# A mixture-of-experts layer: x of expert 0 in two transfers, of the even and of the odd partitions

## The chip, the cores and the metric

The kernel runs on one core of a Trainium2 chip. The core has five engines that run their own instruction streams: TensorE (PE) multiplies matrices, VectorE (DVE) and ScalarE (ACT) do elementwise work, GpSimd (POOL) and SyncE (SP) here mainly issue transfers. Sixteen DMA engines move data between the chip's memory (HBM) and the on-chip SBUF, which has 128 partitions. The metric is the time of one execution in device microseconds: 179.32 us before, the median of 3 runs (179.29 to 179.36).

## The reference

```python
def setup_inputs():
    n_experts, capacity, hidden, expert_hidden = 8, 256, 512, 2048
    ...
def reference(x, w1, w2):
    h = np.matmul(x, w1)
    h = np.maximum(h, 0)
    return np.matmul(h, w2).astype(np.float32)
```

For each of 8 experts, x is 256 x 512, w1 512 x 2048 and w2 2048 x 512, all float32. x is 4.2 MB in all, the weights are 67.1 MB and the result is 4.2 MB.

## The kernel before, in words

The kernel has no planner: each engine's instructions are written out, and semaphores order the engines.

**Loads.** GpSimd casts to bfloat16 while it loads. It first issues x of experts 4 to 7 (`x_c`, L154), then w1 and w2, one transfer of 4.2 MB of float32 for each matrix (`load_w1` L144, `load_w2` L149; the last w2 in two pieces, L151 and L152). There are two buffers for w1 and two for w2; a transfer for a later expert waits until the expert before it in that buffer has been used. SyncE loads x of experts 0 to 3 as float32 into `x_f` in three transfers at L97: expert 0, then experts 1 and 2 together, then expert 3. Each has a semaphore of its own, `s_x[0]` to `s_x[2]`; a landed transfer adds 16 to it. Expert 0 is laid out with rows 2p and 2p+1 in partition p, so each partition gets 4 KB that lie in one piece in HBM.

**The barrier.** After these three issues the kernel closes its tile context (L103 and L104), which puts a barrier over all engines there. What GpSimd, ACT, DVE and PE do for the kernel comes behind that barrier, GpSimd's transfers too.

**Turning x.** For each pair of experts `take_x` runs on two engines at once: DVE takes the experts with b = 0 and ACT those with b = 1. Each waits for its x, casts it to bfloat16 in `x_b` (`cast`, L187), lets TensorE transpose the 16 blocks of the pair (L285) and copies the result to `xe` (L203, L213, L216). TensorE waits for both casts before it transposes a pair. DVE's first cast is the only reader of x of expert 0; its wait is the one in `take_x` with r = 0 and b = 0.

**The layers.** For each pair of experts TensorE runs layer 1 of both (L301; ReLU on DVE L235 and ACT L233) and then layer 2 of both (L321; copies to `out_sb` at L244). TensorE takes one unit of the semaphore `t_w` before each expert's layer 1 and before layer 2. SyncE gives these units: it waits for a weight's landing (L121 for w1, L130, L132 and L133 for w2) and then adds to `t_w`.

**Stores.** SyncE stores experts 0 to 5 in one transfer at L126, expert 6 and expert 7 in one each at L136, and at the end waits for all three landings (L332).

Of the kernel before, what the change touches and what calls it, by code (L numbers as in the profile page):

```python
# [9 lines left out]
def kernel(  # L10
# [8 lines left out]
    P = 128  # L19
# [25 lines left out]
    x_r = x.rearrange("e (p m) k -> p e m k", m=MT)  # L45
# [4 lines left out]
    x_f = nc.alloc_sbuf_tensor("x_f", [P, G, MT, H], f32)  # L50
# [16 lines left out]
    s_x = [sem(f"s_x{i}") for i in range(3)]  # L67
# [21 lines left out]
    sp, pool, act, dve, pe = nc.sync, nc.gpsimd, nc.scalar, nc.vector, nc.tensor  # L89
# [3 lines left out]

    def load_x(eng, e, n, src, i):
        ins = eng.dma_start(x_f[:, e:e + n], src).then_inc(s_x[i], 16)  # L97
        return ins.ins.name

    tc.no_tile_sem_insts.add(load_x(sp, 0, 1, x_r[:, :1], 0))  # L100
    tc.no_tile_sem_insts.add(load_x(sp, 1, 2, x_pair, 1))
    tc.no_tile_sem_insts.add(load_x(sp, G - 1, 1, x_r[:, G - 1:G], 2))
    tc.close()  # L103
    tc.compile()  # L104
# [77 lines left out]
    def cast(eng, r, b):  # L182

        a = 2 * r + b
        src = x_f[:, a] if a < G else x_c[:, MT * (a - G):MT * (a - G + 1)]
        copy = act.copy if eng is act else dve.tensor_copy
        copy(  # L187
            x_b[:, b].rearrange("p (t m) q -> p t m q", m=MT),
            src.rearrange("p m (q t) -> p t m q", t=KT1),
        ).then_inc(t_xb, 1)  # L190

    def take_x(eng, b):
        copy = act.copy if eng is act else dve.tensor_copy
        for r in range(G):
            if r < G // 2:
                eng.wait_ge(s_x[(2 * r + b + 1) // 2], 16)
            elif r == G // 2:
                eng.wait_ge(s_xc, 16)
            cast(eng, r, b)
            eng.wait_ge(s_tr, 2 * r + b + 1)  # L200
            a, n = 2 * r + b, KT1 * C
            if a in (0, G - 1):
                copy(  # L203
                    xe[:, a * n:(a + 1) * n].rearrange("p (j f r) -> p j f r", f=2, r=R),
                    pt[b][:].rearrange("p j (r f) -> p j f r", f=2),
                ).then_inc(s_xe[b], 1)
            else:
                e0, l = (1, 2) if a < G else (G, G)
                f, i = (a - e0) % 2, (a - e0) // 2
                xl = xe[:, e0 * n:(e0 + 2) * n].rearrange(  # L210
                    "p (l j f q i) -> p l j f q i", l=2, j=KT1 * MT, f=2, i=l // 2)
                xp = pt[b][:].rearrange("p j (l q) -> p j l q", l=l)
                ins = copy(xl[:, :, :, f, :, i].rearrange("p l j q -> p j l q"), xp[:, :, :2])  # L213
                if l == G:
                    xl = xe[:, (E - 2) * n:].rearrange("p (l j q f) -> p l j q f", l=2, j=KT1 * MT, f=l)
                    ins = copy(xl[:, :, :, :, a - e0].rearrange("p l j q -> p j l q"), xp[:, :, 2:])  # L216
                ins.then_inc(s_xe[b], 1)
# [41 lines left out]

    act.sem_inc(t_ha, 1)  # L260
    take_x(act, 1)
    layers(act, 1, s_ha, s_oa, t_ha, s_act)

    dve.sem_inc(t_hb, 1)
    take_x(dve, 0)
    layers(dve, 0, s_hb, s_ob, t_hb, s_dve)

# [13 lines left out]
    with pe.Fori(0, G) as _r:  # L281
        take(t_xb, 2)
        for b in range(2):
            for j in range(KT1 * MT):
                ins = pe.transpose(pt[b][:, j], x_b[:, b, j], identity[:])  # L285
            ins.then_inc(s_tr, 1)

    with pe.Fori(0, G) as g:
        with pe.Fori(0, 2) as b:
            xs = ahead(xe, False, g * (4 * KT1 * C) + b * (2 * KT1 * C), [kt * C for kt in range(KT1)], C)  # L290
            take(t_w)
            with pe.Fori(0, NQ) as q:
                for i in range(FB):
# [6 lines left out]
                    for kt in range(KT1):  # L300
                        ins = pe.matmul(  # L301
                            ph[i // 2][:, i % 2, :],
                            ws[i % 2 * KT1 + kt],
                            xs[kt],
                            start=(kt == 0),
                            stop=(kt == KT1 - 1),
                        )
                    if i % 2:
                        ins.then_inc((s_hb, s_ha)[i // 2], 1)
        with pe.Fori(0, 2) as b:  # L310
            for kt in range(KT2):
# [8 lines left out]
                for m in range(MT):  # L320
                    ins = pe.matmul(  # L321
                        po[:, m],
                        hs[(kt - k0) * MT + m],
                        ws[kt - k0],
                        start=(kt == 0),
                        stop=(kt == KT2 - 1),
                    )
# [35 lines left out]
```

## Time and profile before

| what | value |
|---|---|
| median of 3 runs | 179.32 us |
| time of the profiled execution | 179.3 us |
| span of the profiled execution | 177.8 us |
| mean granted TensorE clock | 0.975 |
| PE busy | 129.4 us (73%) |
| DVE, ACT, POOL busy | 40.7, 40.1, 11.1 us |
| HBM read and written | 71.30 MB, 4.19 MB |

The span reaches from the first to the last instruction; the time of the execution has 1.5 us more around it. In the profile, PEld is TensorE's loading of weights, and SPq stands for SyncE's queue of instructions. GB/s of the DMA engines are counted by what is written, so a transfer that casts float32 to bfloat16 shows half of the bytes that it reads.

### The profile page before, as it was taken

Reading aid. Unit: us, or ns where it says so; the run is one execution under the profiler, and the core shown is the slowest. Engines: PE = TensorE matmul, PEld = TensorE weight load, DVE = VectorE, ACT = ScalarE, POOL = GpSimd, SP = SyncE. Lnnn points to the kernel's source line nnn. Section 1 sums busy time; section 2 is a strip of 40 time slices with the busy share of each in tenths; the row PEclk is TensorE's granted clock in tenths of the full one; section 3 lists DMA queues with packets and bytes.
Section 4 is the critical chain, followed back from the end, with each engine's and each line's share of the span. In section 5 each row is a group of like instructions: output and inputs, shape, how many; then the busy total and the mean of one; then the engine's idle time right before and its main releaser. Section 6 shows DMA issues by size and latency. Waiting matters only on the chain. (4 is left out here: it accounts for less than half of the span.)

```text
span 177.8 us, 2369 instructions
## 1 busy us (share of the span) xinstructions
PE 129.4 (73%) x824; PEld 87.8 (49%) x832; DVE 40.7 (23%) x56; ACT 40.1 (23%) x57; POOL 11.1 (6%) x24
## 2 busy tenths in 40 slices
PE   0034399897939697888769695979496695979890
PEld 0033388793413296773324485954142594944330
DVE  0142553331030333330200331320303132310100
ACT  2464543221020222130200222220202121310101
POOL 2600000101010001000010101010100200000000
PEclk9999999999996999999969999999999999999997
DMA  5999999999999999999999999999998999999998
GB/s 227 334 240 203 236 210 203 236 210 203 236 210 203 236 210 203 236 210 203 236 214 199 236 214 199 236 214 199 236 221 192 236 221 192 236 192 217 298 431 337
DMA packets 3712, 40.90 MB, mean 230 GB/s; under 512 B 384, under 2 KB 384, under 8 KB 1024
## 3 DMA queue, kind: packets, MB, share of 16 engines
q0 software_dynamic: 2592, 34.60, 91.5%
q1 hardware_dynamic: 1120, 6.29, 8.6%
HBM read 71.30 MB, written 4.19 MB: 425 GB/s over the span
## 5 line engine op out<-in xcount | busy, mean ns | idle before, releaser
L301 PE MATMUL pt_h<-xe,w_sb 128*128 x512 | 62.8, 276 | 12.5 <-PEq L92 12.4
L321 PE MATMUL pt_o<-w_sb,ht_sb 128*128 x248 | 59.4, 395 | 14.4 <-PEq L92 14.0
L301 PEld LDWEIGHTS pt_h<-xe,w_sb 128*128 x512 | 56.0, 146 | 19.9 <-issue 19.6
L321 PEld LDWEIGHTS pt_o<-w_sb,ht_sb 128*128 x256 | 25.3, 101 | 47.5 <-issue 21.0
L235 DVE TENSOR_SCALAR ht_sb<-pt_h 128x512 bf16<-128x512 f32 x32 | 22.1, 692 | 47.6 <-PE pt_h L301 47.6
L233 ACT ACTIVATE ht_sb<-pt_h 128x512 bf16<-128x512 f32 x32 | 19.1, 597 | 52.6 <-PE pt_h L301 52.6
L244 DVE COPY out_sb<-pt_o 64x512 f32 (+1 forms) x14 | 9.6, 689 | 68.9 <-PE pt_o L321 68.8
L244 ACT COPY out_sb<-pt_o 64x512 f32 (+1 forms) x14 | 8.1, 580 | 67.8 <-PE pt_o L321 67.7
L285 PE MATMUL pt_tr<-identity,x_b 128*128 128x128 bf16 x64 | 7.5, 310 | 16.9 <-PEq L92 16.9
L285 PEld LDWEIGHTS pt_tr<-identity,x_b 128*128 128x128 bf16 x64 | 6.5, 144 | 17.6 <-issue 17.6
L144 POOL DMA_DIRECT2D w_sb<-in_w_dram x8 | 5.0, 624 | 66.3 <-ACTq L237 66.3
L149 POOL DMA_DIRECT2D w_sb<-in_w_dram x7 | 3.7, 532 | 49.0 <-ACT out_sb L244 48.9
L187 ACT CAST x_b<-x_f 128x1024 bf16<-128x1024 f32 x2 | 4.0, 1988 | 2.3 <-DMA x_f<-in_x_dram 2.3
L213 DVE COPY xe<-pt_tr 128x512 bf16<-128x512 bf16 (+1 forms) x3 | 2.1, 715 | 7.9 <-PE pt_tr L285 7.9
L213 ACT COPY xe<-pt_tr 128x512 bf16<-128x512 bf16 (+1 forms) x3 | 2.5, 828 | 6.1 <-PE pt_tr L285 6.1
L187 DVE CAST x_b<-x_f 128x1024 bf16<-128x1024 f32 x2 | 2.1, 1067 | 4.1 <-DMA x_f<-in_x_dram 4.1
L216 ACT COPY xe<-pt_tr 128x512 bf16<-128x512 bf16 x2 | 2.7, 1336 | 0.0
L216 DVE COPY xe<-pt_tr 128x512 bf16<-128x512 bf16 x2 | 2.6, 1301 | 0.0
L203 DVE COPY xe<-pt_tr 128x1024 bf16<-128x1024 bf16 x1 | 1.2, 1225 | 4.5 <-PE pt_tr L285 4.5
L187 ACT COPY x_b<-x_c 128x1024 bf16<-128x1024 bf16 x2 | 2.3, 1132 | 0.0
L187 ACT ACT_TABLE_LOAD x1 | 1.3, 1283 | 2.9 <-PEq L104 2.9
L203 ACT COPY xe<-pt_tr 128x1024 bf16<-128x1024 bf16 x1 | 1.0, 1012 | 2.0 <-PE pt_tr L285 2.0
(10 smaller groups left out, 4.0 us busy)
## 6 DMA issues: line engine op xcount, KB each, us to landing
w_sb<-in_w_dram POOLq DMA_DIRECT2D x15, 2048.0 KB, 29.8
out_dram<-out_sb SPq DMA_DIRECT2D x1, 3072.0 KB, 9.8
w_sb<-in_w_dram POOLq DMA_DIRECT2D x1, 1152.0 KB, 25.7
x_f<-in_x_dram SPq DMA_DIRECT2D x2, 512.0 KB, 5.1
x_f<-in_x_dram SPq DMA_DIRECT2D x1, 1024.0 KB, 5.3
x_c<-in_x_dram POOLq DMA_DIRECT2D x1, 1024.0 KB, 9.4
out_dram<-out_sb SPq DMA_DIRECT2D x2, 512.0 KB, 6.1
w_sb<-in_w_dram POOLq DMA_DIRECT2D x1, 896.0 KB, 29.4
```

Source lines behind the costliest of these rows:

```text
L144: pool.dma_start(w1_k[:, e % 2 * KT1:(e % 2 + 1) * KT1], w1_r[e]).then_inc(s_w1[e], 16)
L149: pool.dma_start(w2_k[:, k:k + KT2], w2_r[e]).then_inc(s_w2[e], 16)
L187: copy(x_b[:, b].rearrange("p (t m) q -> p t m q", m=MT), src.rearrange("p m (q t) -> p t m q", t=KT1),).then_inc(t_xb, 1)
L203: copy(xe[:, a * n:(a + 1) * n].rearrange("p (j f r) -> p j f r", f=2, r=R), pt[b][:].rearrange("p j (r f) -> p j f r", f=2),).then_inc(s_ ...
L213: ins = copy(xl[:, :, :, f, :, i].rearrange("p l j q -> p j l q"), xp[:, :, :2])
L216: ins = copy(xl[:, :, :, :, a - e0].rearrange("p l j q -> p j l q"), xp[:, :, 2:])
L233: act.activation(dst, ph[half][:], relu).then_inc(t_h, 1)
L235: dve.tensor_relu(dst, ph[half][:]).then_inc(t_h, 1)
L244: ins = copy(dst, src)
L285: ins = pe.transpose(pt[b][:, j], x_b[:, b, j], identity[:])
L301: ins = pe.matmul(ph[i // 2][:, i % 2, :], ws[i % 2 * KT1 + kt], xs[kt], start=(kt == 0), stop=(kt == KT1 - 1),)
L321: ins = pe.matmul(po[:, m], hs[(kt - k0) * MT + m], ws[kt - k0], start=(kt == 0), stop=(kt == KT2 - 1),)
```

## The change

Expert 0's x comes in two transfers of 64 partitions each: first the even partitions 0, 2, 4, ..., then the odd ones. Both add to the same semaphore, and DVE's first wait asks for 32 in place of 16. Nothing else is edited.

```diff
-    def load_x(eng, e, n, src, i):
-        ins = eng.dma_start(x_f[:, e:e + n], src).then_inc(s_x[i], 16)
+    def load_x(eng, e, n, src, i, rows=slice(0, P)):
+        ins = eng.dma_start(x_f[rows, e:e + n], src[rows]).then_inc(s_x[i], 16)
         return ins.ins.name
 
-    tc.no_tile_sem_insts.add(load_x(sp, 0, 1, x_r[:, :1], 0))
+    for odd in range(2):
+        tc.no_tile_sem_insts.add(load_x(sp, 0, 1, x_r[:, :1], 0, slice(odd, P, 2)))
     tc.no_tile_sem_insts.add(load_x(sp, 1, 2, x_pair, 1))
     tc.no_tile_sem_insts.add(load_x(sp, G - 1, 1, x_r[:, G - 1:G], 2))
...
             if r < G // 2:
-                eng.wait_ge(s_x[(2 * r + b + 1) // 2], 16)
+                eng.wait_ge(s_x[(2 * r + b + 1) // 2], 32 if r + b == 0 else 16)
```

SyncE's instructions before, from the program's start to its stores (a branch stands where the program passes on, at L104 into the barrier):

```order
L358 UNCONDITIONAL_BRANCH
L97 DMA x_f<-in_x_dram 128x1024
L97 DMA x_f<-in_x_dram 128x2048
L97 DMA x_f<-in_x_dram 128x1024
L104 UNCONDITIONAL_BRANCH
L126 DMA out_dram<-out_sb 128x3x2048
L136 DMA out_dram<-out_sb 128x1024 x2
```

The same of the changed kernel, whose lines below L97 stand one further down:

```order
L359 UNCONDITIONAL_BRANCH
L97 DMA x_f<-in_x_dram 64x1024 x2
L97 DMA x_f<-in_x_dram 128x2048
L97 DMA x_f<-in_x_dram 128x1024
L105 UNCONDITIONAL_BRANCH
L127 DMA out_dram<-out_sb 128x3x2048
L137 DMA out_dram<-out_sb 128x1024 x2
```

In place of the first transfer stand two of 64 rows, so the other two transfers of x and the barrier come one instruction later on SyncE. The other engines have the same instructions in the same order.

## Rows read from the trace of the kernel before

**Rows 1.** The page: TensorE's busy time, DMA by slice (tenths busy), the queues.
```profile
PE 129.4 (73%) x824; PEld 87.8 (49%) x832; DVE 40.7 (23%) x56; ACT 40.1 (23%) x57; POOL 11.1 (6%) x24
...
DMA  5999999999999999999999999999998999999998
DMA packets 3712, 40.90 MB, mean 230 GB/s; under 512 B 384, under 2 KB 384, under 8 KB 1024
...
q0 software_dynamic: 2592, 34.60, 91.5%
q1 hardware_dynamic: 1120, 6.29, 8.6%
HBM read 71.30 MB, written 4.19 MB: 425 GB/s over the span
```

**Rows 2.** Windows of the span; the last columns are DMA share and GB/s.
```profile
core 0: us, PE busy (x) PEld busy (x) DVE busy (x) ACT busy (x) POOL busy (x), PEclk, DMA share, GB/s
1.60:1.80 0.20, 0.00 (x0) 0.00 (x0) 0.00 (x0) 0.00 (x0) 0.00 (x0) 1.00 0.22 41
1.80:2.00 0.20, 0.00 (x0) 0.00 (x0) 0.00 (x0) 0.00 (x0) 0.00 (x0) 1.00 0.93 164
2.00:2.20 0.20, 0.00 (x0) 0.00 (x0) 0.00 (x0) 0.00 (x0) 0.00 (x0) 1.00 0.75 205
2.20:2.40 0.20, 0.00 (x0) 0.00 (x0) 0.00 (x0) 0.00 (x0) 0.00 (x0) 1.00 0.76 307
2.40:2.60 0.20, 0.00 (x0) 0.00 (x0) 0.00 (x0) 0.00 (x0) 0.00 (x0) 1.00 1.00 389
2.60:2.80 0.20, 0.00 (x0) 0.00 (x0) 0.00 (x0) 0.00 (x0) 0.00 (x0) 1.00 0.92 369
2.80:6.80 4.00, 0.00 (x0) 0.00 (x0) 1.07 (x1) 1.53 (x2) 3.08 (x6) 1.00 1.02 414
6.80:7.20 0.40, 0.00 (x0) 0.00 (x0) 0.00 (x0) 0.40 (x1) 0.40 (x1) 1.00 1.83 533
7.20:7.60 0.40, 0.00 (x0) 0.00 (x0) 0.00 (x0) 0.40 (x1) 0.40 (x2) 1.00 0.76 164
7.60:160.00 152.40, 117.14 (x771) 82.50 (x778) 38.25 (x53) 36.62 (x54) 7.03 (x14) 0.98 1.02 216
160.00:166.80 6.80, 5.87 (x27) 2.55 (x27) 0.69 (x1) 0.58 (x1) 0.00 (x0) 1.00 1.04 217
166.80:167.20 0.40, 0.40 (x3) 0.20 (x2) 0.00 (x0) 0.00 (x0) 0.00 (x0) 1.00 0.72 215
167.20:167.60 0.40, 0.40 (x4) 0.20 (x2) 0.00 (x0) 0.00 (x0) 0.00 (x0) 1.00 0.97 389
167.60:177.00 9.40, 5.60 (x26) 2.35 (x24) 0.69 (x1) 0.59 (x1) 0.00 (x0) 0.93 1.00 421
177.00:177.40 0.40, 0.00 (x0) 0.00 (x0) 0.00 (x0) 0.00 (x0) 0.00 (x0) 0.50 0.14 51
```

**Rows 3.** Waits of SyncE: us in total, times, longest.
```profile
SPq L121 <- DMA w_sb<-in_w_dram: 86.9, 8, 19.7
SPq L130 <- DMA w_sb<-in_w_dram: 42.4, 7, 9.7
```

**Rows 4.** Timeline near the end: start us, us, engine, instruction.
```profile
165.46 0.40 SPq L126 DMA_DIRECT2D out_dram<-out_sb  x1
```

**Rows 5.** Timeline of the start.
```profile
0.74 1.33 SPq L97 DMA_DIRECT2D x_f<-in_x_dram  x3
2.94 1.28 ACT L187 ACT_TABLE_LOAD   x1 [2.94 <-PEq L104]
3.36 0.66 POOL L154 DMA_DIRECT2D x_c<-in_x_dram  x1 [2.91 <-POOLq L104]
4.11 1.07 DVE L187 CAST x_b<-x_f 128x1024 bf16<-128x1024 f32 x1 [4.11 <-DMA x_f<-in_x_dram]
6.55 1.99 ACT L187 CAST x_b<-x_f 128x1024 bf16<-128x1024 f32 x1 [2.33 <-DMA x_f<-in_x_dram]
```

**Rows 6.** Lines L97 and L136: duration ns min/median/max, first and last start.
```profile
L97 SPq DMA_DIRECT2D x_f<-in_x_dram x3: 383/421/424, 0.7 to 1.6; - x3
L136 SPq DMA_DIRECT2D out_dram<-out_sb x2: 332/341/350, 168.0 to 174.0; - x2
```

## The prediction

> **What bounds the kernel now.** I read the head of the page first. TensorE is busy for 73% of the span, while the line of the DMA engines shows 9 tenths or more in every slice but the first, which has 5, and two later ones, which have 8 [rows 1]. The two queues together took 91.5% + 8.6% of sixteen engines' time, and HBM moved 425 GB/s over the whole span [rows 1]. That is a kernel bound by its transfers; the chain of waits on the page names TensorE at the end, but it doesn't follow a store's landing, so I didn't rest on it.
>
> The second view was the table of windows. The reader is to see where the stream begins, whether it ever thins out, and where it ends. The first bytes move between 1.60 and 1.80 us, the rate then climbs for about a microsecond, and from there on the share stays at 1.00 to 1.04 in every long window, up to 177.0 us [rows 2]. (A packet is booked whole where it starts, so windows of 0.2 to 0.4 us scatter, even above 1.) Weights show as 216 GB/s, since two bytes are written for four that are read; x and the results, which are not cast, show as 414 to 421 GB/s [rows 2].
>
> The third was SyncE's list of waits, since SyncE passes each landing on to TensorE: 86.9 us and 42.4 us of waiting for weights at the two places that hand them over [rows 3]. So TensorE waits for weights all along, and the end follows the stream.
>
> Last, the end itself. The large store is issued at 165.46 us [rows 4], and its higher rate appears from 167.2 us on [rows 2]. The first transfer of all, issued at 0.74 us [rows 5], moves bytes at 1.6 to 1.8, thus 0.86 to 1.06 us after its issue. By that measure the store was ready at about 166.5 us and stood behind weights for 0.7 us. The last store is issued at 174.0 us [rows 6], ready at 175.1, and the 3.67 MB ahead of it, at 421 GB/s from about 167.2, last until 175.9. So compute has 0.7 to 0.8 us of slack at both places. The time is therefore the first byte, plus the time that all bytes take, plus any gap. The change moves the same bytes; only the first microseconds can move the time.
>
> **The change part by part.** SyncE issued three transfers, 383 to 424 ns each, starting between 0.7 and 1.6 us, so 0.45 us apart [rows 6]. Now it issues four.
>
> *First half of x.* Issued at 0.74 as before. The start is the one thing that can get better. In the six windows from 1.60 to 2.80 us the engines moved (41 + 164 + 205 + 307 + 389 + 369) x 0.2 = 295 KB [rows 2]; at 421 GB/s that takes 0.70 us, so 0.50 us of the 1.2 us were lost to the climb. A transfer of 64 rows in place of 128 may bring the later engines their first rows sooner, or may change nothing. Bounds: from 0.50 us gained to 0; and on the other side a second climb of 0.50 us, if the second half pays one in the open. The trace shows how a second transfer follows a first: x of experts 1 and 2 follows x of expert 0 inside the window 2.80 to 6.80, which runs at 414 GB/s throughout [rows 2]. The nearest row therefore says no second climb, and I take a gain of 0.1 us, a fifth of what the climb costs.
>
> *Second half.* Issued at 0.74 + 0.45 = 1.19, ready at 1.19 + 1.06 = 2.25. By 2.60 the engines have moved 221 KB [rows 2] and the first half has 262 KB, so it lasts until about 2.7. The second half is ready 0.45 us before that, so no gap: 0.
>
> *One more completion.* The 384 packets under 512 B [rows 1] are 16 for each of 24 transfers, so each engine gets one small packet more. In the 4.00 us at 414 GB/s instead of 421 the shortfall is 0.07 us, over two transfers' ends; thus at most 0.03 us. I take 0.01.
>
> *Later issues on SyncE.* x of experts 1 and 2 is issued 0.45 us later, at 1.64, and ready at 2.70. Of the first transfer's 524 KB, 295 are moved by 2.80 and the other 229 take 0.54 us, so it lasts to 3.3: 0.6 us to spare. The fourth transfer follows likewise. Cost 0.
>
> *What stands behind SyncE.* The barrier at L104 waits until SyncE has issued its transfers; GpSimd's first transfer comes at 3.36 us and ACT's table load at 2.94 [rows 5], and both go to 0.45 us later. GpSimd's queue carries all weights, so this is the place where the extra issue could bite. Its first transfer, the other half of x, shows no bytes until SyncE's 2.10 MB are through: 295 KB by 2.80, the other 1.80 MB at 414 GB/s until 7.15, and there the rate falls to that of cast data [rows 2]. It was issued by 3.36 + 0.66 = 4.02 [rows 5]. So it became ready somewhere between 4.02 and 7.15, and a delay of 0.45 us costs 0 to 0.45 us. The nearest row is the 1.06 us from issue to bytes on SyncE: ready at about 4.4, then 4.9, and hidden by 2.3 us. I take 0. ACT's load ends at 4.7 instead of 4.2, and ACT works first at 6.55 [rows 5]: 0.
>
> *The wait for 32.* VectorE alone waits for both halves; it begins its cast at 4.11 us and takes 1.07, while ACT's cast of the next x runs from 6.55 for 1.99, and TensorE's first transposes wait for both casts [rows 5]. So x of expert 0 could land 3.3 us later without holding TensorE. Nothing can start on one half alone, so an earlier first half buys nothing there.
>
> Sum: 179.3 of the profiled execution - 0.1 + 0.01 = 179.2. The median of the runs shown is 179.32, so the profiled execution stands for them.
>
> [...]
>
> **The rivals.**
>
> *A. GpSimd's queue opens late.* If its first transfer was ready only just before 7.15 us, the 0.45 us of later barrier stand open as a gap before all weights. For it: its bytes begin right where SyncE's end, which is also what a transfer that is just in time would look like. Against it: 3.1 us from the end of an issue would be three times what the row on SyncE shows. Time: 179.3 + 0.45 = 179.75.
>
> *B. Every second partition is slower to write.* If the sixteen engines, given every second row, crowd on half of the paths into SBUF, both halves run at half rate: 524 KB at 210 in place of 421 GB/s costs 1.25 us, and since the stream never pauses, all weights land that much later. It decides from the point where x of expert 0 takes over 0.36 us longer. For it: no transfer of before has this row pattern, so no row excludes it. Against it: the rows span all 128 partitions either way. Time: 180.55.
> [...]
>
> *C. The climb mostly goes.* If the climb of 0.50 us comes from handing out 128 rows over sixteen engines, the half-size first transfer takes most of it away: all engines start together, and the engine that is last at the start isn't last at the end. For it: 164 and 205 GB/s in the first two windows after the first bytes [rows 2]. [...] Time: 179.3 - 0.45 = 178.85.
>
> **How the numbers follow.** A measurement here tells 0.2%, 0.36 us, from no change. The forecast, a change of -0.35 to +0.35 us around -0.1, gets 0.60; its own range is 178.95 to 179.65. C gets 0.22, all of it faster. A gets 0.07 and B 0.09, and 0.02 goes to a gap that I haven't seen; all of that is slower. So faster 0.22, same 0.60, slower 0.18. The range reaches from C's time to A's, 178.8 to 179.75, and leaves out B and a little beyond C.
>
> **What would show it.** In the profile after: four issues at L97, 0.45 us apart; GpSimd's first transfer at 3.8 us; the fall of the rate to that of cast data still at 7.0 to 7.2 us; the wait for the first weights and the end shifted by the same small amount. In the head's windows 295 KB or somewhat more by 2.80. A fall of the rate at 8.4 us would show B; a dip of the share near 7.2 to 7.6 would show A; well over 350 KB by 2.80 would show C. The forecast is wrong if the head shifts by more than 0.36 us, or if the end doesn't follow the head: then the sixteen engines don't move as one.

## The result, and the profile after

| what | before | after |
|---|---|---|
| median of 5 runs, us | 179.29 (179.20 to 179.36) | 181.14 (181.03 to 182.08) |
| ratio with its 95% interval | | 1.0119 [1.0104, 1.0133] |
| profiled execution, us | 179.3 | 182.08 |
| span of it, us | 177.8 | 180.6 |

The change costs 1.85 us. The forecast was 179.2 us and its range ended at 179.75, so it was wrong, and in the direction as well. The profiled execution is the longest of the five; where its excess matters I use the profile of a second run of the same kernel (e1 below, 180.95 us), 0.19 us under the median.

The page of after, for [rows 1]:

```profile
PE 129.7 (72%) x832; PEld 87.6 (49%) x832; DVE 40.7 (23%) x56; ACT 40.1 (22%) x57; POOL 11.1 (6%) x24
...
DMA  4999999999999999999999999999999999999897
...
q0 software_dynamic: 2592, 34.60, 90.1%
q1 hardware_dynamic: 1136, 6.29, 9.0%
HBM read 71.30 MB, written 4.19 MB: 418 GB/s over the span
```

Work and bytes are as before, SyncE's queue has the 16 packets of one more completion (1136 against 1120), and HBM moves 418 in place of 425 GB/s over the span: the loss is time in which the DMA engines move less. The two queues' share of the engines' time goes from 100.1% to 99.1%. On the page only the first slice and two near the end give a hint. The table of windows shows where it is, first in the head, then near the end (columns as in [rows 2]):

```profile
1.60:2.80 1.20, 0.00 (x0) 0.00 (x0) 0.00 (x0) 0.00 (x0) 0.00 (x0) 1.00 0.43 157
2.80:3.60 0.80, 0.00 (x0) 0.00 (x0) 0.00 (x0) 0.00 (x0) 0.00 (x0) 1.00 1.10 358
3.60:4.40 0.80, 0.00 (x0) 0.00 (x0) 0.00 (x0) 0.51 (x1) 0.09 (x1) 1.00 0.61 149
4.40:5.20 0.80, 0.00 (x0) 0.00 (x0) 0.09 (x1) 0.77 (x1) 0.80 (x2) 1.00 0.94 292
5.20:6.00 0.80, 0.00 (x0) 0.00 (x0) 0.80 (x1) 0.00 (x0) 0.80 (x1) 1.00 1.06 317
6.00:6.80 0.80, 0.00 (x0) 0.00 (x0) 0.17 (x1) 0.00 (x0) 0.80 (x2) 1.00 0.71 297
...
167.00:168.00 1.00, 1.00 (x6) 0.30 (x4) 0.03 (x1) 0.00 (x0) 0.00 (x0) 1.00 1.00 208
168.00:169.00 1.00, 0.15 (x1) 0.00 (x1) 0.67 (x1) 0.58 (x1) 0.00 (x0) 1.00 0.53 108
```

Where before moved 414 GB/s throughout from 2.80 to 6.80 [rows 2], after falls to 149 between 3.6 and 4.4 and stays near 300 until 6.8. The five windows from 2.80 to 6.80 add up to 1413 GB/s; at 414 they would be 2070. The difference times 0.8 us is 526 KB, and at 421 GB/s that is 1.25 us. The start itself, 157 in place of 246 GB/s (the sum of the first six windows of [rows 2]), is another 0.25 us. Together these 1.5 us are a mean over the sixteen engines; the last engine of this profile is 2.78 us behind, as its landings show below.

The start of the timeline, for [rows 5], then line L97, for [rows 6]:

```profile
0.74 2.29 SPq L97 DMA_DIRECT2D x_f<-in_x_dram  x4
3.89 1.28 ACT L188 ACT_TABLE_LOAD   x1 [3.89 <-PEq L105]
4.31 0.66 POOL L155 DMA_DIRECT2D x_c<-in_x_dram  x1 [3.86 <-POOLq L105]
5.11 1.06 DVE L188 CAST x_b<-x_f 128x1024 bf16<-128x1024 f32 x1 [5.11 <-DMA x_f<-in_x_dram]
9.43 1.99 ACT L188 CAST x_b<-x_f 128x1024 bf16<-128x1024 f32 x1 [4.26 <-DMA x_f<-in_x_dram]
```

```profile
L97 SPq DMA_DIRECT2D x_f<-in_x_dram x4: 431/562/578, 0.7 to 2.6; - x4
```

Three of the four issues now take 0.55 to 0.58 us and the last takes 0.43, where before all three took 0.38 to 0.42. In the trace the four start at 0.738, 1.347, 1.972 and 2.593 us. So x of experts 1 and 2 is issued at 1.97 and not at 1.64, against 1.18 before, and the barrier opens 0.95 us later and not 0.45. ACT, which waits for x of experts 1 and 2, casts at 9.43 in place of 6.55.

At the other end, SyncE's waits, for [rows 3], and its stores, for [rows 4]:

```profile
SPq L122 <- DMA w_sb<-in_w_dram: 88.9, 8, 21.5
SPq L131 <- DMA w_sb<-in_w_dram: 42.2, 7, 9.7
```

```profile
168.30 0.40 SPq L127 DMA_DIRECT2D out_dram<-out_sb  x1
```

The longest wait, that for the first weights, grew by 1.8 us and begins 0.95 us later, thus 2.75 in all; the large store comes 2.84 us later. So the head's loss goes through to the end whole. The landings by DMA engine in the trace say how. The first weights land on 11 engines at 23.2 to 24.1 us and on the other five at 25.1 to 25.3; before, all sixteen were through at 22.0 to 22.5. Afterwards the stream doesn't pause (DMA share 1.02 from 12 to 160 us, as before), and the five stay behind to the end: the eleven are through with the first weights 1.0 us before the first of the five, and with the last weights again 1.0 us. What waits for a transfer waits for the last of its sixteen landings: ACT's cast of x of experts 1 and 2 begins at 9.43 us, and the last engine lands that transfer at 9.42. On the other eleven the last weights land at 168.6 to 169.4 us, before the store is there: that is the window at 108 GB/s, with ACT and DVE at the copies that the store waits for. The last store lands at 179.6 to 179.8 us on eleven engines and at 180.4 to 180.5 on five (before: 177.3 to 177.7). In e1's profile the last engine gets the first weights 1.6 us later than before and the end is 1.6 us later.

### The profile page after: what moved, and what is told of

It reads as the page before. It is cut to its first block, busy times and chain, and to the rows that moved or that the text cites. A ratio compares the mean times of both kernels' runs of the same rounds, so it can differ in the third digit from the quotient of the medians.

```text
span 180.6 us, 2378 instructions
## 1 busy us (share of the span) xinstructions
PE 129.7 (72%) x832; PEld 87.6 (49%) x832; DVE 40.7 (23%) x56; ACT 40.1 (22%) x57; POOL 11.1 (6%) x24
## 3 DMA queue, kind: packets, MB, share of 16 engines
q1 hardware_dynamic: 1136, 6.29, 9.0%
## 5 line engine op out<-in xcount | busy, mean ns | idle before, releaser
L302 PE MATMUL pt_h<-xe,w_sb 128*128 x512 | 62.7, 276 | 12.7 <-PEq L92 12.6
## 6 DMA issues: line engine op xcount, KB each, us to landing
x_c<-in_x_dram POOLq DMA_DIRECT2D x1, 1024.0 KB, 11.3
```

The costliest lines, as they stand in the source:

```text
L302: ins = pe.matmul(ph[i // 2][:, i % 2, :], ws[i % 2 * KT1 + kt], xs[kt], start=(kt == 0), stop=(kt == KT1 - 1),)
```

## The experiments

Rates of the head, in GB/s, from the table of windows of each profile, and when the transfer of x of experts 1 and 2 ("x12" from here on) is issued:

| kernel | x12 at | 1.6-2.8 | 2.8-3.6 | 3.6-4.4 | 4.4-5.2 | 5.2-6.0 | 6.0-6.8 | median us |
|---|---|---|---|---|---|---|---|---|
| before | 1.18 | 246 | 471 | 399 | 389 | 399 | 410 | 179.29 |
| after | 1.97 | 157 | 358 | 149 | 292 | 317 | 297 | 181.14 |
| e1 after again | 1.97 | 195 | 297 | 220 | 307 | 379 | 369 | 181.75 |
| e2 long issue | 1.34 | 133 | 394 | 440 | 399 | 410 | 374 | 179.66 |
| e3 two by row parity of x | 1.65 | 259 | 312 | 159 | 276 | 276 | 317 | 181.66 |
| e4 lower, upper half | 1.97 | 133 | 333 | 215 | 215 | 440 | 389 | 181.12 |
| e10 x12 on ACT | 0.74 | 143 | 399 | 471 | 353 | 333 | 420 | 179.60 |
| e11 x12 first on SyncE | 0.74 | 157 | 420 | 420 | 384 | 374 | 420 | 179.91 |
| e9 short pause | 1.66 | 242 | 374 | 256 | 287 | 307 | 246 | 182.03 |
| e8 pause | 2.36 | 229 | 323 | 102 | 399 | 410 | 358 | 180.55 |

**The scatter, and the longer issue.** e1 is the changed kernel once more.

> The changed kernel once more, since its first profile fell on the longest of its five executions (182.08 us, span 180.6, where three of five have a span of 179.6). All theories: 181.1 us. What is asked is the profile of a usual execution. If the loss is one thing of varying size, five of sixteen engines again get x of experts 1 and 2 late and end up behind the others, by less than in the first profile (1.0 us between the two groups in the landings of the first weights). If the first profile's late group was an accident on top of the loss, no late group shows and all engines are about 1.8 us behind before.

181.75 us (180.95 to 182.28), ratio 1.0141 [1.0116, 1.0167]. The loss is there again. It scatters by 1.3 us; 13 runs of before on the same chip lie between 179.21 and 179.90. In its profile x12 lands late on all engines, at 6.8 to 8.3 us (before 6.2 to 6.5), and the first weights at 22.7 to 24.1, but no engines form a group apart. So the loss doesn't need the group of five; that group is what the long first profile has on top.

e2 is the kernel before, with the first transfer built without the mark that the program gives to transfers over all 128 partitions:

```diff
+    nc.dge_precook = False
     tc.no_tile_sem_insts.add(load_x(sp, 0, 1, x_r[:, :1], 0))
+    nc.dge_precook = True
```

> The kernel before, with one edit: the first transfer (128 partitions, unchanged in shape and number) is built without the mark that the program gives to transfers over all 128 consecutive partitions and that the two 64-row transfers don't get. Theory L (the long way of issuing is what costs): its issue takes about 0.55 us in place of 0.38, the first bytes come at about 2.2 us in place of 1.8, time at least 179.3 + 0.4 = 179.7, and up to 180.7 if the rows of the next transfer come late as well. Theory N (a fourth transfer in the queue costs) and theory P (64 rows on every second partition cost): 179.3, first bytes at 1.8.

179.66 us, ratio 1.0017 [1.0007, 1.0027]. The issue takes 0.54 us in place of 0.38, like one of 64 rows (0.55 to 0.58 in after), and the next one, which keeps its mark, 0.57. First bytes come at 2.12 in place of 1.79 us and the rest of the head is full (374 to 440 GB/s from 2.8 to 6.8 us). So without the mark a transfer of 128 rows showed the issue time of one of 64 rows, the one behind it took longer too, as in after, and the longer issue by itself cost 0.37 us here.

**Which part of the change.** e3 splits x of expert 0 over its two rows per partition, so both transfers have 128 partitions:

```diff
+        ins = sp.dma_start(x_f[:, 0, odd], x_r[:, 0, odd]).then_inc(s_x[0], 16)
```

> x of expert 0 in two transfers that both go over all 128 partitions, each half of a partition's 4 KB; both keep the mark. Four transfers as in the changed kernel. Theory L: issues 0.45 us apart as before, first bytes at 1.8 us, no late engines; 179.3 us, or up to 179.75 if GpSimd's delay of 0.45 us behind the barrier is not covered. Theory N: like the changed kernel, 180.5 to 181.1. Theory P: as theory L.

181.66 us (179.94 to 182.12), ratio 1.0103 [1.0042, 1.0164]. The issues take 0.38 and 0.42 us, x12 comes at 1.65, just where I had put it for the change, and the gap is there all the same. So the step fails even with my own issue time, and no even and odd partitions are needed for it.

e4 takes the lower and the upper 64 partitions:

```diff
+        tc.no_tile_sem_insts.add(load_x(sp, 0, 1, x_r[:, :1], 0, slice(R * odd, R * odd + R)))
```

> x of expert 0 in the lower and the upper 64 partitions in place of the even and the odd ones: 64 consecutive rows, also without the mark. Theory L: the same as the changed kernel in issue times (0.55 to 0.58 us, 0.61 apart) and first bytes (2.2 us), 181.1 us, plus up to 1.2 us if a half of the partitions is written at half rate. Theory P (every second partition): better than the changed kernel, near 179.5. Theory N: 181.1.

181.12 us (180.75 to 182.41), ratio 1.0116 [1.0069, 1.0163], as after. Which partitions a half takes decides nothing here.

e5 is e3 with the last two transfers in one, in the layout of expert 0, so that SyncE has three transfers again:

```diff
-    tc.no_tile_sem_insts.add(load_x(sp, 1, 2, x_pair, 1))
-    tc.no_tile_sem_insts.add(load_x(sp, G - 1, 1, x_r[:, G - 1:G], 2))
+    tc.no_tile_sem_insts.add(load_x(sp, 1, 3, x_r[:, 1:G], 1))
```

> x of expert 0 in two transfers over all 128 partitions (as in e3), then x of experts 1 to 3 in one; three transfers on SyncE in all, with the simple row layout for experts 1 and 2 and their copies adapted to it. Theory Q (the third transfer on one queue gets its rows late, whatever it is): the rate falls between 3.2 and 6 us as in e3, 180.5 to 181.7. Theory N (it takes four transfers): 179.3, no late engines. Theory G (a transfer that is issued when the engines already move data gets its rows late; here the third, at 1.65 us): as theory Q.

182.15 us (181.73 to 182.42), ratio 1.0160 [1.0141, 1.0180]. Timeline and windows of e5:

```profile
1.65 0.43 SPq L97 DMA_DIRECT2D x_f<-in_x_dram  x1
...
3.36 0.66 POOL L155 DMA_DIRECT2D x_c<-in_x_dram  x1 [2.91 <-POOLq L105]
```

```profile
3.60:4.40 0.80, 0.00 (x0) 0.00 (x0) 0.00 (x0) 0.63 (x1) 0.80 (x2) 1.00 0.51 74
4.40:5.20 0.80, 0.00 (x0) 0.00 (x0) 0.41 (x1) 0.00 (x0) 0.80 (x3) 1.00 1.41 143
```

GpSimd starts at 3.36 as before and there is no fourth transfer; the gap is the deepest so far. What is left is that the transfer behind x of expert 0 is issued at 1.65 us. That transfer is larger here and has rows of 4 KB in place of 8, so the size of this loss isn't compared with the others.

e6 is e3 with x of expert 3 issued on ACT:

```diff
+    tc.no_tile_sem_insts.add(load_x(act, G - 1, 1, x_r[:, G - 1:G], 2))
```

> As e3, but x of expert 3 is issued by ACT on its own queue; SyncE keeps the two halves of x of expert 0 and x of experts 1 and 2. Theory Q: x of experts 1 and 2 is still the third on its queue: late engines, 180.5 to 181.7. Theory N, if it counts one queue: 179.3; if it counts all queues: 181. Theory G: late, since that transfer is still issued at 1.65 us.

179.59 us, ratio 1.0016 [1.0006, 1.0025]. x12 is again third on SyncE, at 1.65, and there is no gap: 366 to 446 GB/s from 2.8 to 6.8 us, where e3 fell to 159. Expert 3's rows, issued at 0.74, lie ahead meanwhile. So x12 at third place and at 1.65 cost no more than 0.32 us here; that it need only be there when the rows ahead of it run out is my reading of e3 and e6. The 0.32 us that stay go with a slower start (111 GB/s from 1.6 to 2.8), with first bytes at 2.06 us although its issues are short (0.40 us on ACT, 0.42 for x12).

e7 has the two transfers of e3 on SyncE and ACT side by side:

```diff
+        ins = (sp, act)[odd].dma_start(x_f[:, 0, odd], x_r[:, 0, odd]).then_inc(s_x[0], 16)
```

> As e3, but the second half of x of expert 0 is issued by ACT at the same time as SyncE issues the first half. SyncE has three transfers, and x of experts 1 and 2 is its second, issued at 1.18 us as before. Theory Q and theory G: no late engines, 179.3. Theory N over all queues: 181.

179.15 us (179.11 to 179.87), ratio 0.9995 [0.9983, 1.0007]. x12 goes out at 1.18 as before, and nothing is lost or gained: no measurable difference from before, and the fastest kernel with x of expert 0 in two.

**The change itself, with x12 early.** e10 is after with one word changed (the edit below), e11 is after with the unchanged line of x12 moved ahead of the two halves:

```diff
-    tc.no_tile_sem_insts.add(load_x(sp, 1, 2, x_pair, 1))
+    tc.no_tile_sem_insts.add(load_x(act, 1, 2, x_pair, 1))
```

> The changed kernel, but x of experts 1 and 2 is issued by ACT at 0.74 us, beside the even half on SyncE. The even and the odd half stay as they are. Theories W and W+: its rows are there before the halves run out, so only the later first bytes remain (2.1 in place of 1.8 us): 179.7, at most 180.0. Theory P (the even and odd partitions themselves cost): near 181.1.

> The changed kernel with the same four transfers on SyncE in another order: x of experts 1 and 2 first, then the even half, the odd half, x of expert 3. The first transfer is the largest (2.5 us of data at 420 GB/s), so the next two are issued 3 us before the engines need them. Theories W and W+: no gap at the start, first bytes at 1.8 us; 179.2 to 179.6, as GpSimd's transfers come some 0.8 us later than before. Theory N (four transfers) and theory P: 180.5 to 181.1.

e10: 179.60 us (179.44 to 179.96), ratio 1.0018 [1.0008, 1.0028]. e11: 179.91 us (179.62 to 180.92), ratio 1.0034 [1.0018, 1.0050]. Windows of e10:

```profile
1.60:2.80 1.20, 0.00 (x0) 0.00 (x0) 0.00 (x0) 0.00 (x0) 0.00 (x0) 1.00 0.68 143
2.80:3.60 0.80, 0.00 (x0) 0.00 (x0) 0.00 (x0) 0.04 (x1) 0.00 (x0) 1.00 0.94 399
3.60:4.40 0.80, 0.00 (x0) 0.00 (x0) 0.00 (x0) 0.80 (x1) 0.42 (x1) 1.00 1.11 471
```

Both keep the even and the odd half, the long issues and four transfers, and GpSimd is late in both (3.98 and 4.24 us). In e10 the start is slower: (246 - 143) x 1.2 us at 421 GB/s is 0.29 us, and 0.31 were measured. The expectation had another reason for that, first bytes at 2.1 us; they come at 1.78, from ACT's transfer, and the trace shows 8 KB rows that take up to 1.28 us there. By 2.80 us e10 has moved no more than after (143 against 157 GB/s), so the 1.54 us between the two kernels arise behind that, where x12 comes late in after. e11 lies above its expected 179.6; by it 1.23 us would be x12's.

**How late is too late.** In e14, e9, e8 and e15 the kernel before waits between its first and its second transfer, by 3, 8, 20 and 44 increments of a semaphore that nobody reads:

```diff
+    s_pad = sem("s_pad")
+    for _ in range(20):
+        sp.sem_inc(s_pad, 1)
```

> The kernel before, with 20 semaphore updates on SyncE between the first and the second transfer, some 0.5 to 1 us, so that x of experts 1 and 2 is issued at 1.7 to 2.1 us, as late as in the changed kernel or e3, while it stays the second of three. Theory G: its rows come late, the rate falls between 3.2 and 6 us, 180.5 or more. Theory Q and theory N: the second transfer is ready by about 3.3 us and no engine is late; the rest of the loss is GpSimd's delay of the same 0.5 to 1 us, 179.3 to 179.8.

> As e8 with 8 semaphore updates in place of 20: x of experts 1 and 2 is issued at about 1.65 us, as in e3, but is the second of three. e8 lost 1.25 us for 1.18 us of later issue. Theory W (the rows of a transfer come some 2.1 us after its issue, so each later microsecond of issue is lost once the transfer ahead has run out, and nothing else): 179.3 + 0.5 = 179.8. Theory W+ (an engine that has run out of rows is served slowly from then on, whatever the number of transfers): as e3, 180.5 to 181.7.

> As e9 with 3 semaphore updates in place of 8: x of experts 1 and 2 issued at about 1.36 us, 0.18 later than before. The rows of the kernel before come just in time or with a margin. Theory J (just in time): some engines are late already, 179.8 or more. Theory M (a margin of over 0.2 us): 179.3.

> As e8 with 44 semaphore updates in place of 20: x of experts 1 and 2 issued at 3.4 to 3.8 us, when all engines have long run out of rows or are about to. Theory W (only the later issue counts): 179.3 + 2.3 to 2.7 = 181.6 to 182.0, and all engines equally late as in e8. Theory C (rows that are written while engines run out of them come slowest, so e9 is the worst place): the loss is no more than the later issue, first packets not over 0.5 us long, and 181.6 or less.

| kernel | x12 at | later by | median us | ratio | x12's landings over the engines |
|---|---|---|---|---|---|
| before | 1.18 | | 179.29 | | 6.18 to 6.53 |
| e14 | 1.36 | 0.18 | 179.34 | 1.0002 [0.9984, 1.0020] | 6.2 to 6.56, one 7.14 |
| e9 | 1.66 | 0.48 | 182.03 | 1.0139 [1.0116, 1.0161] | nine 6.20 to 6.54, seven 7.39 to 10.03 |
| e8 | 2.36 | 1.18 | 180.55 | 1.0075 [1.0058, 1.0091] | 6.87 to 7.68 |
| e15 | 3.77 | 2.59 | 181.72 | 1.0126 [1.0110, 1.0143] | 8.29 to 8.59 |

A delay of 0.48 us, with no other edit, costs 2.74 us. The pause also moves what stands behind x12: in e9 x of expert 3 and GpSimd's first transfer come 0.39 us later. In e5 GpSimd is not late and the gap is there too. Windows of e9, then of e15:

```profile
3.60:4.40 0.80, 0.00 (x0) 0.00 (x0) 0.28 (x1) 0.80 (x1) 0.65 (x1) 1.00 0.69 256
4.40:5.20 0.80, 0.00 (x0) 0.00 (x0) 0.78 (x1) 0.21 (x1) 0.80 (x2) 1.00 1.02 287
5.20:6.00 0.80, 0.00 (x0) 0.00 (x0) 0.00 (x0) 0.00 (x0) 0.80 (x3) 1.00 0.99 307
6.00:6.80 0.80, 0.00 (x0) 0.00 (x0) 0.00 (x0) 0.00 (x0) 0.44 (x3) 1.00 0.73 246
```

```profile
3.60:4.40 0.80, 0.00 (x0) 0.00 (x0) 0.00 (x0) 0.00 (x0) 0.00 (x0) 1.00 0.00 0
4.40:5.20 0.80, 0.00 (x0) 0.00 (x0) 0.00 (x0) 0.00 (x0) 0.00 (x0) 1.00 0.72 82
5.20:6.00 0.80, 0.00 (x0) 0.00 (x0) 0.49 (x1) 0.55 (x1) 0.14 (x1) 1.00 0.55 225
6.00:6.80 0.80, 0.00 (x0) 0.00 (x0) 0.57 (x1) 0.73 (x1) 0.80 (x2) 1.00 1.04 440
```

e15 shows a transfer that comes to idle engines (0 GB/s from 3.6 to 4.4): issued at 3.77, first bytes at 4.73 (0.96 us later), full rate from about 5.8, 2.0 us after its issue. In the trace eight engines start their first row 0.96 to 1.05 us after the issue and the other eight 1.71 to 1.79 us after it. All engines are then equally late, and its loss of 2.43 us is about its delay of 2.59 us; so it is in e8, 1.26 against 1.18. In e9 nine engines have x12 as early as before, and the other seven 0.9 to 3.5 us after them; the loss is nearly six times the delay. What sets those seven apart is not shown. After, e3 and e5 have uneven landings too: in after 11 engines have x12 at 6.8 to 7.9 and five at 9.2 to 9.4. There five first rows start at 5.1 to 5.4 us, 3.2 to 3.5 us after the issue, and take 1.40 to 1.65 us each, against 0.31 for most rows of x12. In e4 and e1 all engines are late and none stand apart (7.3 to 8.3 and 6.8 to 8.3). That e8 with the longer delay loses less than e9 rests on both intervals, which lie apart.

**GpSimd's later start.** To look at it with x12 in time, e12 leaves x of expert 0 whole and splits x of expert 3, the last of SyncE's transfers; e13 does that and moves these two behind the barrier:

```diff
+    for odd in range(2):
+        tc.no_tile_sem_insts.add(load_x(sp, G - 1, 1, x_r[:, G - 1:G], 2, slice(odd, P, 2)))
...
-                eng.wait_ge(s_x[(2 * r + b + 1) // 2], 16)
+                eng.wait_ge(s_x[(2 * r + b + 1) // 2], 32 if r + b == 2 else 16)
```

> x of expert 0 in one transfer as before; instead x of expert 3, the last on SyncE's queue, comes in an even and an odd half (both without the mark). Four transfers, two of them of every second partition, but each has the transfers ahead of it as cover: needed at 5.8 and 6.5 us, issued at 1.65 and 2.25. Theories W and W+: 179.2 to 179.6. Theories N and P: 180.5 to 181.1.

> e12 with one edit: the two halves of x of expert 3 are issued behind the barrier, so GpSimd's first transfer comes at about 2.9 us in place of 4.39. e12 lost 1.45 us; its rate fell between 7.6 and 9.2 us, right where GpSimd's first rows are due. Theory B (the issues ahead of the barrier delay GpSimd, and that is e12's whole loss): no fall there, 179.2 to 179.5. Theory P (halves of every second partition cost by themselves): still 180.5 or more.

e12: 180.74 us (180.35 to 181.01), ratio 1.0067 [1.0044, 1.0091]. e13: 179.76 us (179.61 to 179.82), ratio 1.0021 [1.0011, 1.0031]. Timeline and windows of e12:

```profile
4.39 0.88 POOL L155 DMA_DIRECT2D x_c<-in_x_dram  x1 [3.95 <-POOLq L105]
```

```profile
6.80:7.60 0.80, 0.00 (x0) 0.00 (x0) 0.00 (x0) 0.80 (x1) 0.67 (x2) 1.00 1.72 384
7.60:8.40 0.80, 0.00 (x0) 0.00 (x0) 0.00 (x0) 0.80 (x1) 0.69 (x2) 1.00 0.51 67
8.40:9.20 0.80, 0.45 (x5) 0.48 (x6) 0.00 (x0) 0.21 (x1) 0.00 (x0) 1.00 0.74 154
```

Here SyncE's rows are in time (x12 lands at 6.2 to 6.6 us and x of expert 3 by 8.2, before by 8.4), and the gap stands where GpSimd's rows should begin: the rate is that of cast data only from about 9.2 us on (208 GB/s until 12 us), 4.8 us after the issue at 4.39. In e13 GpSimd is issued at 2.88 and 1 us of the loss is gone; under 0.5 us stay, between what the theories B and P of its expectation say and nearer to B. But e13 also issues x of expert 3 later (2.38 and 2.95 us), and e11 has no such gap with GpSimd's issue at 4.24, only 0.15 us before that of e12. Windows of e11:

```profile
6.80:7.60 0.80, 0.00 (x0) 0.00 (x0) 0.79 (x1) 0.69 (x1) 0.77 (x1) 1.00 1.36 461
7.60:8.40 0.80, 0.36 (x4) 0.39 (x5) 0.29 (x1) 0.00 (x0) 0.80 (x2) 1.00 1.10 225
```

So no fixed time from GpSimd's issue to its full stream follows, and that its delay makes e12's 1.45 us is argued and not shown. In after GpSimd's issue comes at 4.31, its first rows move at 8.0 us while x is still moving, and the windows from 6.8 to 9.2 us (353, 369 and 261 GB/s) have no gap.

## Why the prediction was wrong, point by point

**What held.** The kernel is bound by its transfers, and only the first microseconds could move the time. VectorE's later cast (5.11 in place of 4.11) doesn't count: in e10 it comes at 7.12, and the whole loss is 0.31 us. The extra completion added 16 packets of no visible cost.

**The step that failed** is the one on the later issues: "ready at 2.70", "0.6 us to spare", "Cost 0". It took a transfer's readiness as the time from issue to the first bytes, 1.06 us. That is when the first row moves, not when all engines have theirs: e15 shows 0.96 us from the issue to the first bytes and 2.0 us to the full rate, with half of the engines at their first row only after 1.7 us. With 2.0 us, x12 issued at 1.64 would have been ready at 3.64, and x of expert 0 lasted by my own sum to 3.3. The climb of a microsecond behind the first bytes was in [rows 2] and in the text; I charged it to the first transfer only, because the second followed without a dip. That proved merely that 1.18 us was early enough, not by how much: e14 is unharmed at 1.36 within its interval of about 0.3 us, though one engine of its profile is late and one run took 180.51 us; e9 at 1.66 is not.

**The price of that lateness** was mis-sized too: by my sum 0.3 us of lateness would have cost 0.3. e9 shows 2.74 us for 0.48, and its engines do not move as one: seven have x12 at 7.39 to 10.03 us and the other nine by 6.54, and ACT's cast waited 5.4 us for the last. The prediction named engines that don't move as one among its signs of being wrong.

**The issue's length.** 0.45 us apart, taken from transfers of 128 partitions [rows 6], was 0.61 to 0.63 behind those of 64. e3 shows that the shorter one would have made no difference to the sign.

**The start.** Instead of -0.1 us it is about +0.3: e2, which has the long issue alone, loses 0.37 with first bytes at 2.12 us, and after has them at 2.22, against 1.79 before. A late first byte is not the only way to a slow start, as e10 and e11 show (first bytes at 1.78 and 1.75, yet 143 and 157 GB/s).

**The rivals.** C falls: no kernel with a half-size first transfer climbs faster (157 and 195 GB/s against 246; e3, with the short issue, 259, which is 0.04 us, but e5 with the same two transfers 224). B falls: e3 and e4 lose as much without the pattern, and e10 and e11, which have it, move 333 to 471 GB/s from 2.8 to 6.8 us, far from the 210 of half rate, and lose 0.3 and 0.6. A is not what decides in after: e5 has the gap with GpSimd at 3.36 as before, and e11 has none at 4.24. In e12 GpSimd's rows were not there 3.2 us after their issue (67 GB/s), so the 1.06 us that I took over from SyncE were too short for them; how much cover they had before stays open. A fixed price of one more transfer doesn't make the 1.85 us either: two transfers in place of one cost 0 us in e7 (each over all 128 partitions) and 0.3 in e10 (partition halves), where x12 is early.

**What stays open.** Why some engines get x12 so much later than its delay, and why the shorter delay of e9 costs more than the longer ones. The runs show it (e9 against e8 and e15) without its cause. Why e12 has a gap at GpSimd's rows and e11 has none is open too. The sum of after, 0.3 for the start and 1.5 for x12, rests on e2 and e10; in e10 x12 is also on another queue, and e11, on the same queue, leaves 0.6 and not 0.3.

## What to carry to other kernels

Where a queue of transfers starts a kernel that is bound by its transfers, look at what stands behind an issue more: here that made the difference between 1.85 us (after) and 0.31 (e10). Compare the time at which the rows ahead run out with the next issue plus the whole climb to the full rate (here 2.0 us on SyncE by e15; for GpSimd the runs give no one time), not plus the time to the first byte (0.96 us there). That a transfer of before follows its forerunner without a dip says only that it was early enough; the margin has to be worked out or tried (here 0.18 us more did no harm that the runs could show, and 0.48 did). If a split is needed, putting its second part on another engine's queue cost nothing here (e7); the larger transfer ahead still cost 0.6 us (e11).

## What the runs showed of the hardware that I had not expected

- On SyncE a transfer of 64 partitions took 0.52 to 0.65 us to issue (after, e4, e10 to e13) and one of 128 partitions 0.33 to 0.43 (before, after, e8, e9), but 0.57 to 0.72 right behind one of 64 partitions (after, e10, e11) or behind the long issue of e2.
- The loss did not grow with the delay: 0.18, 0.48, 1.18 and 2.59 us of it cost 0.05, 2.74, 1.26 and 2.43 us; the first is within the noise.
- In e15 the first 8 KB rows took 1.07 to 1.30 us on eight of the idle engines, against 0.31 in the running stream; on the other eight they began 0.7 us later and took 0.31 to 0.40.
- In after the last rows of x come among GpSimd's rows: from 10.9 to 12.7 us they start five at a time, 0.78 us apart, where a row of x takes 0.17 us and one of GpSimd's 0.62. SyncE's last x lands at 13.6 to 13.8 us on five engines, and at 8.4 to 11.3 on the others. Before, SyncE's last sixteen rows start at 6.99 to 7.28 us and GpSimd's first sixteen at 7.09 to 7.43.
